# Rotation tables of a state-space scan built once for all groups, and two projections moved behind the scan

## The chip, the core and the metric

The kernel runs on one core of a Trainium2 chip. Its engines have queues of their own, each run in order: TensorE (PE; matmuls), VectorE (DVE; element-wise work and the scan), ScalarE (ACT; copies, casts and functions from tables), GpSimd (POOL; a second element-wise engine) and SyncE (SP; it issues the DMA transfers). Engines wait for each other by semaphores. The metric is device time in microseconds (us) for one execution; lower is better.

## The reference

A hybrid layer is followed by a second block (feed-forward layers, a convolution with an RWKV scan, latent attention), all in fp32 on 512 positions of width 1024. Only the hybrid layer is touched:

```python
proj = jnp.einsum("bld,de->ble", rms_norm(x, pre_g), w_in)
conv_in, z_c, u_s, z_s, g_c, g_s = jnp.split(proj, IN_OFFSETS, axis=-1)
ca, cb = jnp.split(conv_in, 2, axis=-1)
cu = causal_depthwise_conv(ca * jax.nn.sigmoid(cb), conv_w, conv_b)      # 31 taps
cu = jax.nn.silu(layer_norm(cu, conv_ln_g, conv_ln_b))
conv_out = (cu * jax.nn.silu(z_c)) @ w_conv_out
y = jax.nn.gelu(s5_mimo(u_s, ...))       # per group g: s_t = Abar s_(t-1) + Bbar u_t, y = Re(C s) + D u
y = y * jax.nn.sigmoid(y @ w_glu + b_glu)
ssm_out = (y * jax.nn.silu(z_s)) @ w_ssm_out
merged = jax.nn.sigmoid(g_c) * conv_out + jax.nn.sigmoid(g_s) * ssm_out
out = x + rms_norm(merged @ w_out, post_g)
```

The state-space scan (S5) has 32 groups of 16 channels with 64 complex states. Abar is mag * exp(i * angle), with an angle per state and group.

## The kernel before

Activations lie with channels on the 128 partitions and the 512 positions along the free axis. Every weight matrix comes as fp32 and is split into a high and a low part, so that a product is three matmuls. `wload` does this by 1024 columns: SP fetches `raw`, ACT casts it to `wh` (L235), DVE subtracts to get `wl` (L236); there are two buffers of each. `mm3` (L247 to L249) runs xh*wh, xl*wh and xh*wl. One projection, `proj`, is 2048 columns, two halves of 24 matmuls of 512 columns each. The bank of a half is free for the next use when its result has been read.

The hybrid layer is `block1`. Its input projections are named by step in two strings, ORDER_A and ORDER_B, and the steps are issued in that order; a scheduler then places instructions on the engines by priority, in which a step's class (`B1_CLASS`, `B1_PRIO`) can lower it: only the convolutions on ACT and POOL (class C) are lower.

```python
ORDER_A = "p0 P1 T z0 c0 u0 u1 s0 p3 t1 Q0 Q1 q0 c3 P2 t2 s1 Q2 q1 p5 z1 c5 P4 t4 Q3 q2 P6 t6 q3 P7 t7"
ORDER_B = "z2 z3 y0 g0 g1 g2 y1 y2 y3 g3 G L g4 g5 g6 S0 g7 S1 C0 C1 C2 C3 C4 C5 C6 C7"
```

- p and P: a projection of 128 gated convolution channels. After p the convolution runs as c on ACT (a product with each tap, L758) and POOL (its addition, L759). After P the gated result `cp` (DVE, L718) is split into `cph` (ACT, L724) and `cpl` (DVE, L725), and t runs the convolution on PE as a Toeplitz product of 4 weight chunks, 24 matmuls of 256 columns each (L741 to L743).
- u: the scan's input, stored to DRAM by SP and read back as `us` in the layout of the scan. s and z: the gates z_s and z_c, a projection with Silu (z at L792). Both kinds of gate and the squares of x at the start take buffers of a pool `b1z`.
- T (`s5_tables`): quantities of all 32 groups, 32 elements per partition each, among them the powers of Abar and, for the rotation, cosine and sine of the angle times 2^i, by doubling eight times with ten instructions each (L462 to L475; `s5x` and `s5t` are its tiles).
- Q (`s5_pre`), for a quarter q of 8 groups: outer products on POOL (`t`, `w`, L503 and L506), the rotation tables `rc` and `rsn` (cosine and sine of k times the angle for k below 64: six doublings of six DVE instructions, L521 to L526, with 8 to 256 elements), transposes (PE, L531), the kernel of the first 8 steps (PE, L540, then `kt`), the diagonal D added to `kt` group by group (DVE, L545), and 16 transfers that place `kt` in `tz`.
- q (`s5_main`): `us` from DRAM, product with `m` (PE, L571), rotation by the tables (DVE, L577 to L579), the scan (L581), rotation back (L583 on PE, L587 to L589 on DVE), product with `tz` and `w` (PE, L593 and L594).
- Behind the scan: y (gelu), g (gates), G (the product with w_glu), L (layer norm of the convolution, gate z_c), S and C (output products).

Of the kernel before, what the change touches and what calls it, by code (L numbers as in the profile page):

```python
# [341 lines left out]
def s5_tables(P, mp):  # L342
# [119 lines left out]
    for i in range(8):  # L462
        w, u1, u2 = tmp(), tmp(), tmp()
        c2, s2 = (small(), small()) if i >= 2 else (tmp(), tmp())
# [4 lines left out]
        tt(u1, c2, c2, ALU.mult)  # L469
        tt(u2, s2, s2, ALU.mult)  # L470
        tt(w, u1, u2, ALU.add)
        V.tensor_scalar(out=w, in0=w, scalar1=-0.5, scalar2=1.5, op0=ALU.mult, op1=ALU.add)
# [1523 lines left out]
```

## Time and profile before

| | us |
|---|---|
| median of 3 runs | 2741.04 (2734.41 to 2743.03) |
| profiled execution, its own time | 2744.4 |
| span of its trace | 2742.7 |
| PE busy | 2610.5 (95% of the span) |
| DVE busy | 1447.9 (53%) |
| ACT busy | 950.4 (35%) |
| POOL busy | 511.4 (19%) |

The page cuts the span in 40 slices of 68.6 us and gives each engine's busy share in tenths; a window gives busy us between two times. A row of a timeline has the start, the duration, the engine, line and operation, and in brackets the idle time of the engine before it and what ended that. A group of a line has the count, the busy us, the mean ns, and the idle time before. PEclk and the number behind the engines in a window are the granted TensorE clock, as a share of full. The names and lines are those of the kernel before.

### The profile page before, as it was taken

What the parts mean: (1) busy time and instruction counts of PE and PEld (TensorE: products, weight loads), DVE (VectorE), ACT (ScalarE), POOL (GpSimd) and SP (SyncE); (2) the same over time, 40 slices, a digit from 0 to 9 for tenths busy, and PEclk for the clock granted to TensorE, in tenths of its full rate; (3) what the DMA queues carried; (4) which work ended last, traced back from release to release, by engine and by line L of the source; (5) the groups of instructions that cost most, each with busy time, mean ns of one, the idle gap of its engine ahead of it and who ended that gap; (6) DMA issues with size and microseconds to landing.
All of it is one profiled execution on the core that took longest, in us unless ns stands there. A gap on an engine that the chain in (4) does not pass through costs nothing.

```text
span 2742.7 us, 32329 instructions
## 1 busy us (share of the span) xinstructions
PE 2610.5 (95%) x12836; PEld 2092.4 (76%) x12836; DVE 1447.9 (53%) x2064; ACT 950.4 (35%) x1351; POOL 511.4 (19%) x382
## 2 busy tenths in 40 slices
PE   6688799998999999999999999999999999999999
PEld 4567678886888876787678888888888666788887
DVE  9967643636434448743464344443444755643443
ACT  4354444434222343222242233322233454432231
POOL 5687501014000044332010000100001221100000
PEclk8889799998999999999999999999999889999999
DMA  3222232332233342213222332322324312132323
GB/s 111 74 85 90 74 124 88 108 115 70 95 96 102 96 139 72 64 57 106 67 85 95 98 99 91 102 95 90 107 84 138 112 41 62 50 100 87 106 95 105
DMA packets 116071, 251.87 MB, mean 92 GB/s; under 512 B 44176, under 2 KB 53008, under 8 KB 115920
## 3 DMA queue, kind: packets, MB, share of 16 engines
q1 hardware_dynamic: 115664, 249.00, 28.9%
q8 instruction: 100, 1.64, 0.3%
q0 software_dynamic: 256, 0.81, 0.1%
q14 instruction: 51, 0.42, 0.1%
HBM read 235.21 MB, written 13.37 MB: 91 GB/s over the span
## 4 chain that ended last, share of the span: by engine, by line
PE 82%; DVE 12%; DMA 1%; issue 1%; ACT 1%; POOL 1%; SPq 1%; DVEq 0%; ACTq 0%; POOLq 0%
PE bank L247 23%; PE bank L249 23%; PE bank L248 23%; PE bank L1871 2%; DVE wl L236 2%; DVE s5x L357 1%; POOL acc L264 1%; SPq L548 1%; PE bank L1423 1%; PE bank L1227 0%; DVE ra L525 0%; PE bank L742 0%; PE bank L743 0%; DMA s<-nd 0%; DVE rc L523 0%
## 5 line engine op out<-in xcount | busy, mean ns | idle before, releaser
L235 ACT CAST wh<-raw 128x1024 fp32r<-128x1024 f32 (+1 forms) x452 | 437.2, 969 | 1268.1 <-PE bank L248 948.4
L249 PE MATMUL bank<-xh,wl 128*128 128x512 f32 (+1 forms) x2144 | 843.0, 394 | 30.0 <-DVE wl L236 30.0
L248 PE MATMUL bank<-xl,wh 128*128 128x512 f32 (+1 forms) x2144 | 842.8, 393 | 15.6 <-DVE xl L925 6.9
L247 PE MATMUL bank<-xh,wh 128*128 128x512 f32 (+1 forms) x2144 | 838.2, 392 | 18.5 <-ACT wh L235 7.8
L236 DVE TENSOR_TENSOR wl<-raw,wh 128x1024 fp32r<-128x1024 f32 (+1 forms) x418 | 481.9, 1154 | 484.3 <-ACT wh L235 482.9
L249 PEld LDWEIGHTS bank<-xh,wl 128*128 128x128 f32 x2144 | 408.9, 191 | 125.6 <-DVE wl L236 33.7
L247 PEld LDWEIGHTS bank<-xh,wh 128*128 128x128 f32 x2144 | 408.0, 191 | 109.2 <-ACT wh L235 11.7
L248 PEld LDWEIGHTS bank<-xl,wh 128*128 128x128 f32 x2144 | 408.5, 191 | 106.2 <-DVE xl L925 7.8
L264 POOL TENSOR_TENSOR acc<-acc,sq 128x512 f32<-128x512 f32 x54 | 81.4, 1507 | 1326.9 <-ACT sq L263 1325.8
L249 PE MATMUL bank<-mh,wl 128*128 128x512 f32 x704 | 274.6, 390 | 0.0
L248 PE MATMUL bank<-ml,wh 128*128 128x512 f32 x704 | 274.3, 390 | 0.0
L247 PE MATMUL bank<-mh,wh 128*128 128x512 f32 x704 | 274.1, 389 | 0.0
L323 DVE TENSOR_TENSOR up<-bank,rs 128x512 f32<-128x512 f32 x88 | 60.8, 691 | 266.8 <-PE bank L249 266.8
L249 PEld LDWEIGHTS bank<-mh,wl 128*128 128x128 f32 x704 | 132.1, 188 | 33.2 <-DVE wl L236 1.7
L319 DVE TENSOR_TENSOR gp<-bank,rs 128x512 f32<-128x512 f32 x88 | 60.8, 691 | 179.7 <-PE bank L249 179.7
L248 PEld LDWEIGHTS bank<-ml,wh 128*128 128x128 f32 x704 | 132.1, 188 | 27.9
L247 PEld LDWEIGHTS bank<-mh,wh 128*128 128x128 f32 x704 | 132.2, 188 | 25.6
L759 POOL TENSOR_TENSOR xa<-xa,cw 128x512 f32<-128x512 f32 x90 | 129.1, 1435 | 55.1 <-ACT cw L758 52.5
L236 POOL TENSOR_TENSOR wl<-raw,wh 128x1024 fp32r<-128x1024 f32 x34 | 82.8, 2435 | 145.6 <-ACT wh L235 145.1
L758 ACT ACTIVATE cw<-cu,hcw 128x512 f32<-128x512 f32 x90 | 63.7, 720 | 37.5 <-POOL xa L759 37.3
L253 ACT CAST mh<-m 128x512 fp32r<-128x512 f32 x88 | 54.9, 625 | 61.5 <-DVE m L325 61.5
L1871 PE MATMUL bank<-s,s 128*128 128x256 f32 (+3 forms) x192 | 71.6, 431 | 0.4 <-ACT s L1878 0.4
(651 smaller groups left out, 3032.9 us busy)
## 6 DMA issues: line engine op xcount, KB each, us to landing
raw<-in_ffn_gu_dram SPq DMA_DIRECT2D x176, 512.0 KB, 3.4
raw<-in_ffn_dn_dram SPq DMA_DIRECT2D x64, 512.0 KB, 3.6
raw<-in_w_in_dram SPq DMA_DIRECT2D x46, 512.0 KB, 3.5
raw<-in_even_in_dram SPq DMA_DIRECT2D x26, 512.0 KB, 3.6
raw<-in_ffn_dn_dram SPq DMA_DIRECT2D x64, 192.0 KB, 3.2
raw<-in_conv_dram SPq DMA_DIRECT2D x20, 512.0 KB, 3.8
xa<-in_xT_dram SPq DMA_DIRECT2D x16, 256.0 KB, 4.1
raw<-in_w_co_dram SPq DMA_DIRECT2D x8, 512.0 KB, 3.3
```

Source lines behind the costliest of these rows:

```text
L235: nc.scalar.copy(h[:, :m], raw[:, :m])
L236: self.wlo.tensor_tensor(out=l[:, :m], in0=raw[:, :m], in1=h[:, :m].bitcast(F32), op=ALU.subtract)
L247: self.nc.tensor.matmul(ps, h[i][:, s], xh[k], start=a, stop=False)
L248: self.nc.tensor.matmul(ps, h[i][:, s], xl[k], start=False, stop=False)
L249: last = self.nc.tensor.matmul(ps, l[i][:, s], xh[k], start=False, stop=b)
L253: self.nc.scalar.copy(hi, src)
L264: nc.gpsimd.tensor_tensor(out=acc, in0=acc, in1=sq, op=ALU.add)
L319: nc.vector.tensor_tensor(out=gp, in0=pg, in1=rs, op=ALU.mult)
L323: nc.vector.tensor_tensor(out=up, in0=pu, in1=rs, op=ALU.mult)
L758: A.activation(w, cu[:, j:j + T], AF.Copy, scale=hcw[:, 31 * k + j:31 * k + j + 1])
L759: GP.tensor_tensor(out=y, in0=y, in1=w, op=ALU.add)
L1871: MM(ps[:, 0:N], x, y, start=m == 0, stop=False)
```

## The change

The doubling of the base angles goes. In its place the angle r (with its sign) is multiplied by 8, 16, ... 256 in six small copies on ACT, reduced to one turn in eight DVE instructions on all six at once, and given to Sin twice. The rotation tables of all 32 groups are built by a new step R, `s5_rot`, once, in two tiles of 2048 elements: six doublings, the later ones in parts of 512 elements, 42 DVE instructions where the four quarters had 144. The diagonal is spread once into `idd`, and each half quarter adds it in one instruction (8 instead of 32). In the orders, z0 and z1 leave ORDER_A and stand at the head of ORDER_B; steps in ORDER_A are rearranged around R0. The pool `b1z` has 4 buffers instead of 8 and the pool of the later steps, `b1z2`, 8 instead of 4; `s5x` has 8 instead of 12.

```diff
@@ s5_tables
-    ssn = small()
-    V.tensor_scalar(out=ssn, in0=sn, scalar1=sgn, scalar2=None, op0=ALU.mult)
-    rot = []
-    c, s = cs, ssn
-    for i in range(8):
...
-        tt(u1, c, c, ALU.mult)
-        tt(u2, s, s, ALU.mult)
-        tt(c2, u1, u2, ALU.subtract)
-        V.scalar_tensor_tensor(out=s2, in0=c, scalar=2.0, in1=s, op0=ALU.mult, op1=ALU.mult)
...
-        tt(c2, c2, w, ALU.mult)
-        tt(s2, s2, w, ALU.mult)
...
+    rsg = small()
+    V.tensor_scalar(out=rsg, in0=r, scalar1=sgn, scalar2=None, op0=ALU.mult)
+    ang, nn, aa = (P.t(n)[:, 0:192].rearrange("p (i g) -> p i g", i=6) for n in ("ang", "nn", "aa"))
+    for i in range(6):
+        nc.scalar.activation(ang[:, i], rsg, AF.Copy, scale=2.0 ** (i + 3))
+    V.tensor_scalar(out=nn, in0=ang, scalar1=1.0 / TWO_PI, scalar2=MAGIC, op0=ALU.mult, op1=ALU.add)
+    V.tensor_scalar(out=nn, in0=nn, scalar1=MAGIC, scalar2=None, op0=ALU.subtract)
+    for cst in (PI_C1, PI_C2, PI_C3):
+        V.scalar_tensor_tensor(out=ang, in0=nn, scalar=-cst, in1=ang, op0=ALU.mult, op1=ALU.add)
+    V.tensor_scalar(out=ang, in0=ang, scalar1=PI_CLAMP, scalar2=-PI_CLAMP, op0=ALU.min, op1=ALU.max)
+    V.scalar_tensor_tensor(out=aa, in0=ang, scalar=-1.0, in1=ang, op0=ALU.mult, op1=ALU.max)
+    rs6, rc6 = (sm.tile([128, 6, 32], F32, name=n) for n in ("rs6", "rc6"))
+    nc.scalar.activation(rs6, ang, AF.Sin)
+    nc.scalar.activation(rc6, aa, AF.Sin, scale=-1.0, bias=halfpi)
+    rot = [(rc6[:, i], rs6[:, i]) for i in range(6)]
+    idd = sm.tile([16, 32, 16], F32, name="idd")
...
+def s5_rot(P, tb):
+    V = P.nc.vector
+    c, s = (P.q4.tile([128, 2048], F32, name=n).rearrange("p (g k) -> p g k", g=32) for n in ("rc", "rsn"))
+    V.memset(c[:, :, 0:1], 1.0)
+    V.memset(s[:, :, 0:1], 0.0)
+    ta, tb_ = P.t("ra"), P.t("rb")
+    for i in range(6):
+        m = 1 << i
+        n = min(32, 512 // m)
+        for g0 in range(0, 32, n):
+            g = slice(g0, g0 + n)
+            cq, sq = (a[:, g].unsqueeze(2).to_broadcast([128, n, m]) for a in tb["rot"][i])
+            A, B = (x[:, 0:n * m].rearrange("p (g k) -> p g k", g=n) for x in (ta, tb_))
+            V.tensor_tensor(out=A, in0=c[:, g, 0:m], in1=cq, op=ALU.mult)
+            V.tensor_tensor(out=B, in0=s[:, g, 0:m], in1=sq, op=ALU.mult)
+            V.tensor_tensor(out=c[:, g, m:2 * m], in0=A, in1=B, op=ALU.subtract)
+            V.tensor_tensor(out=A, in0=s[:, g, 0:m], in1=cq, op=ALU.mult)
+            V.tensor_tensor(out=B, in0=c[:, g, 0:m], in1=sq, op=ALU.mult)
+            V.tensor_tensor(out=s[:, g, m:2 * m], in0=A, in1=B, op=ALU.add)
+    tb["cs"] = c, s
@@ s5_pre
-    for i in range(6):
-        m = 1 << i
...
-        RE.tensor_tensor(out=A, in0=c[:, :, 0:m], in1=cq, op=ALU.mult)
...
-            V.scalar_tensor_tensor(out=kt[:, i, 0:16], in0=P.ident[0:16, 0:16], scalar=tb["dd"][:, g:g + 1],
-                                   in1=kt[:, i, 0:16], op0=ALU.mult, op1=ALU.add)
+        g4 = slice(8 * q + 4 * hf, 8 * q + 4 * hf + 4)
+        V.tensor_tensor(out=kt[:, :, 0:16], in0=kt[:, :, 0:16], in1=tb["idd"][:, g4], op=ALU.add)
@@ block1
-        zp = E(tc.tile_pool(name="b1z", bufs=8))
+        zp = E(tc.tile_pool(name="b1z", bufs=4))
...
-        pools["z"] = E(tc.tile_pool(name="b1z2", bufs=4))
+        pools["z"] = E(tc.tile_pool(name="b1z2", bufs=8))
...
-ORDER_A = "p0 P1 T z0 c0 u0 u1 s0 p3 t1 Q0 Q1 q0 c3 P2 t2 s1 Q2 q1 p5 z1 c5 P4 t4 Q3 q2 P6 t6 q3 P7 t7"
-ORDER_B = "z2 z3 y0 g0 g1 g2 y1 y2 y3 g3 G L g4 g5 g6 S0 g7 S1 C0 C1 C2 C3 C4 C5 C6 C7"
+ORDER_A = "p0 P1 T c0 u0 u1 p3 c3 Q0 t1 s0 R0 P2 Q1 t2 q0 p5 c5 s1 Q2 P4 q1 t4 Q3 P6 q2 t6 P7 q3 t7"
+ORDER_B = "z0 z1 z2 z3 y0 g0 g1 g2 y1 y2 y3 g3 G L g4 g5 g6 S0 g7 S1 C0 C1 C2 C3 C4 C5 C6 C7"
```

What the scheduler makes of it is shown at three places. In these rows a name's number is the tile's, and the lines of the changed kernel are one to three higher (L462 to L471 and L498 to L503 are new code there).

On ACT, where the convolution of the first pair begins (`xa` is its sum, `cw` a tap's product, `ang` the scaled angles); before:

```order
L755 ACTIVATE xa<-cu,vec,hcw 128x512
L758 ACTIVATE cw<-cu,hcw 128x512 x2
L235 CAST wh<-raw 128x1024
L792 ACT_TABLE_LOAD
L792 ACTIVATE zc<-bank_73 128x512
L724 CAST cph<-cp 128x2x256
L758 ACTIVATE cw<-cu,hcw 128x512
L235 CAST wh<-raw 128x1024
L792 ACTIVATE zc<-bank_74 128x512
```

and changed:

```order
L757 ACTIVATE xa<-cu,vec,hcw 128x512
L760 ACTIVATE cw<-cu,hcw 128x512 x2
L462 ACTIVATE ang<-s5t_495 128x32 x6
L760 ACTIVATE cw<-cu,hcw 128x512
L726 CAST cph<-cp 128x2x256
L235 CAST wh<-raw 128x1024 x2
L470 ACT_TABLE_LOAD
L470 ACTIVATE rs_513<-ang 128x192
```

The results of z0 (`zc`) are gone from here, the scaled angles stand ahead of `cph`, and both next halves of weights stand behind it.

On DVE, where the first rotation tables begin; before (`d` is the scan's decay, spread over the steps):

```order
L521 TENSOR_TENSOR ra<-rc,s5t_530 128x8
L522 TENSOR_TENSOR ra<-rsn,s5t_531 128x8
L558 COPY d_1395<-s5t_491 128x512
L523 TENSOR_TENSOR rc<-ra 128x8 x2
L524 TENSOR_TENSOR ra<-rsn,s5t_530 128x8
L236 TENSOR_TENSOR wl<-raw,wh 128x1024
L525 TENSOR_TENSOR ra<-rc,s5t_531 128x8
```

and changed:

```order
L498 TENSOR_TENSOR ra<-rc,rc_514 128x32
L499 TENSOR_TENSOR rb<-rsn,rs_513 128x32
L560 COPY d_1477<-s5t_491 128x512
L500 TENSOR_TENSOR rc<-ra,rb 128x32
L501 TENSOR_TENSOR ra<-rsn,rc_514 128x32
L502 TENSOR_TENSOR rb<-rc,rs_513 128x32
L236 TENSOR_TENSOR wl<-raw,wh 128x1024
```

The tables of quarters 0 and 1 ran here side by side, 8 elements for each of two; now one set for all groups starts, 32 elements at a time.

On DVE again, at quarter 2 of the scan; before, in the middle of its tables:

```order
L526 TENSOR_TENSOR rsn<-ra 128x8x8
L521 TENSOR_TENSOR ra<-rc,s5t_590 128x8x16
L522 TENSOR_TENSOR ra<-rsn,s5t_591 128x8x16
L236 TENSOR_TENSOR wl<-raw,wh 128x1024
L523 TENSOR_TENSOR rc<-ra 128x8x16
L524 TENSOR_TENSOR ra<-rsn,s5t_590 128x8x16
L525 TENSOR_TENSOR ra<-rc,s5t_591 128x8x16
```

and changed, the whole way from the decay of quarter 2 to its scan:

```order
L560 COPY d_2213<-s5t_491 128x512
L236 TENSOR_TENSOR wl<-raw,wh 128x1024 x3
L547 TENSOR_TENSOR kt<-kt,idd 16x4x16
L236 TENSOR_TENSOR wl<-raw,wh 128x1024
L720 SCALAR_TENSOR_TENSOR cp<-vb,bank_73 64x256 x4
L579 TENSOR_TENSOR vr<-bank_78,rsn 128x512
L580 TENSOR_TENSOR vs<-vs,rc 128x512
L727 TENSOR_TENSOR cpl<-cp,cph 128x2x256
```

No table stands between weight splits any more, and `cp` now stands ahead of the scan's rotation.

## Rows read from the trace of the kernel before

**Rows 1.** Page, part 2: busy tenths in 40 equal slices of the span.
```profile
PE   6688799998999999999999999999999999999999
...
DVE  9967643636434448743464344443444755643443
```

**Rows 2.** Windows: stretch, busy time of each engine (instructions), granted clock, DMA.
```profile
0.00:140.00 140.00, 94.02 (x342) 69.11 (x343) 134.34 (x296) 61.84 (x87) 87.92 (x75) 0.84 0.29 95
140.00:330.00 190.00, 153.58 (x839) 129.82 (x837) 131.71 (x169) 95.39 (x138) 145.50 (x116) 0.85 0.30 87
330.00:400.00 70.00, 61.60 (x347) 54.50 (x348) 31.67 (x41) 26.96 (x39) 2.58 (x2) 0.86 0.34 105
400.00:600.00 200.00, 198.52 (x872) 163.03 (x870) 96.22 (x113) 80.22 (x107) 18.32 (x10) 1.00 0.31 106
```

**Rows 3.** PE's timeline: start, duration, operation, idle time before it and its releaser.
```profile
130.42 0.80 PE L249 MATMUL bank<-xh,wl 128*128 128x512 f32 x1 [12.15 <-DVE wl L236]
...
213.28 0.58 PE L743 MATMUL bank<-cph,wl 128*128 128x256 f32 x1 [9.47 <-DVE wl L236]
...
290.57 0.58 PE L741 MATMUL bank<-cph,wh 128*128 128x256 f32 x1 [9.00 <-ACT cph L724]
...
327.40 0.87 PE L571 MATMUL bank<-us,m 128*128 128x64 f32 x3 [4.47 <-DMA us<-u_dram]
...
369.92 0.58 PE L741 MATMUL bank<-cph,wh 128*128 128x256 f32 x1 [5.81 <-ACT cph L724]
```

**Rows 4.** DVE's groups by line and shape, 0 to 420: count, busy us, mean ns.
```profile
L236 DVE TENSOR_TENSOR wl<-raw,wh 128x1024 fp32r<-128x1024 f32 x54 | 76.1, 1409 | 81.0 <-ACT wh L235 81.0
L545 DVE SCALAR_TENSOR_TENSOR kt<-ident,s5d,kt 16x16 f32<-16x16 f32 x32 | 13.2, 465 | 9.6 <-ACT kt L542 9.5
L357 DVE TENSOR_TENSOR s5x<-s5x 128x32 f32<-128x32 f32 x22 | 12.3, 580 | 0.3
...
L525 DVE TENSOR_TENSOR ra<-rc,s5t 128x8 f32<-128x8 f32 x4 | 5.0, 1261 | 0.0
L579 DVE TENSOR_TENSOR vs<-vs,vr 128x512 f32<-128x512 f32 x4 | 5.6, 1410 | 0.1
...
L578 DVE TENSOR_TENSOR vs<-vs,rc 128x512 f32<-128x512 f32 x4 | 4.1, 1016 | 0.0
...
L808 DVE TENSOR_TENSOR p<-p,y 128x512 f32<-128x512 f32 x4 | 2.8, 690 | 0.1
```

**Rows 5.** Timelines of DVE and POOL at the tables of quarters 2 and 3.
```profile
189.38 1.23 DVE L521 TENSOR_TENSOR ra<-rc,s5t 128x8 f32<-128x8 f32 x1
190.53 0.16 DVE L522 TENSOR_TENSOR ra<-rsn,s5t 128x8 f32<-128x8 f32 x1
...
217.83 0.43 DVE L526 TENSOR_TENSOR rsn<-ra 128x256 f32<-128x256 f32 x1
...
219.37 1.64 POOL L759 TENSOR_TENSOR xa<-xa,cw 128x512 f32<-128x512 f32 x1 [7.42 <-ACT cw L758]
```

**Rows 6.** Timelines of ACT and POOL at the squares of x and a table load.
```profile
16.02 0.61 ACT L663 ACTIVATE sq<-xa 128x512 f32<-128x512 f32 x1
...
60.47 1.28 ACT L792 ACT_TABLE_LOAD   x1
...
8.81 11.46 POOL L665 TENSOR_TENSOR sqa<-sqa,sq 128x512 f32<-128x512 f32 x7 [4.20 <-ACT sq L663]
```

**Rows 7.** PE's timeline where t1 begins, around P6, before P7, at the end.
```profile
143.78 0.28 PE L741 MATMUL bank<-cph,wh 128*128 128x256 f32 x1
...
311.56 0.48 PE L247 MATMUL bank<-xh,wh 128*128 128x512 f32 x1
...
322.54 0.39 PE L249 MATMUL bank<-xh,wl 128*128 128x512 f32 x1
...
352.95 0.48 PE L247 MATMUL bank<-xh,wh 128*128 128x512 f32 x1
...
385.00 0.29 PE L743 MATMUL bank<-cph,wl 128*128 128x256 f32 x1
```

More of the change, by code (lines that the diff above doesn't have):

```diff
@@ L353, in tmp @@
     def tmp(m=1):
-        return sm.tile([128, m, 32] if m > 1 else [128, 32], F32, name="s5x", tag=f"s5x{m}", bufs=12 if m == 1 else 4)
+        return sm.tile([128, m, 32] if m > 1 else [128, 32], F32, name="s5x", tag=f"s5x{m}", bufs=8 if m == 1 else 4)
     def tt(out, a, b, op, e=V):
@@ L457, in s5_tables @@
     tt(mg8, mg8, mg8, ALU.mult)
-    ssn = small()
-    V.tensor_scalar(out=ssn, in0=sn, scalar1=sgn, scalar2=None, op0=ALU.mult)
-    rot = []
-    c, s = cs, ssn
-    for i in range(8):
-        w, u1, u2 = tmp(), tmp(), tmp()
-        c2, s2 = (small(), small()) if i >= 2 else (tmp(), tmp())
-        tt(u1, c, c, ALU.mult)
-        tt(u2, s, s, ALU.mult)
-        tt(c2, u1, u2, ALU.subtract)
-        V.scalar_tensor_tensor(out=s2, in0=c, scalar=2.0, in1=s, op0=ALU.mult, op1=ALU.mult)
[L469 to L472, printed above, removed]
-        tt(c2, c2, w, ALU.mult)
-        tt(s2, s2, w, ALU.mult)
-        c, s = c2, s2
-        if i >= 2:
-            rot.append((c, s))
+    rsg = small()
[14 more added lines that the diff above has]
+    idd = sm.tile([16, 32, 16], F32, name="idd")
+    tt(idd, P.ident[0:16, 0:16].unsqueeze(1).to_broadcast([16, 32, 16]), dd.unsqueeze(2).to_broadcast([16, 32, 16]), ALU.mult)
     prr, nspr = small(8), small(8)
@@ L484, in s5_tables @@
     V.tensor_copy(perm[:, 64:128], P.ident[:, 0:64])
-    return dict(bc=bc, bb=bb, bbs=bbs, dd=dd, prr=prr, nspr=nspr, spr=spr, npi=npi, mg8=mg8, rot=rot, perm=perm)
+    return dict(bc=bc, bb=bb, bbs=bbs, idd=idd, prr=prr, nspr=nspr, spr=spr, npi=npi, mg8=mg8, rot=rot, perm=perm)
+def s5_rot(P, tb):
[18 more added lines that the diff above has]
+    tb["cs"] = c, s
 def s5_pre(P, tb, q):
@@ L542, in s5_pre @@
         nc.scalar.copy(kt.rearrange("p g s -> p (g s)"), ps[0:16, :])
-        for i in range(4):
-            g = 8 * q + 4 * hf + i
-            V.scalar_tensor_tensor(out=kt[:, i, 0:16], in0=P.ident[0:16, 0:16], scalar=tb["dd"][:, g:g + 1],
-                                   in1=kt[:, i, 0:16], op0=ALU.mult, op1=ALU.add)
+        g4 = slice(8 * q + 4 * hf, 8 * q + 4 * hf + 4)
+        V.tensor_tensor(out=kt[:, :, 0:16], in0=kt[:, :, 0:16], in1=tb["idd"][:, g4], op=ALU.add)
         for j in range(8):
             nc.sync.dma_start(tz[16 * j:16 * j + 16, 4 * hf:4 * hf + 4, 16 * j:128], kt[:, :, 0:128 - 16 * j])
-    tb[q] = w2, m1, tz, c, s
+    tb[q] = w2, m1, tz
 def s5_main(P, tb, q, u_dram, y_dram):
@@ L555, in s5_main @@
     gs = slice(8 * q, 8 * q + 8)
-    w2, m1, tz, c, s = tb[q]
+    w2, m1, tz = tb[q]
+    c, s = (a[:, gs] for a in tb["cs"])
     d0 = P.t("d0").rearrange("p (g k) -> p g k", g=8)
@@ L790, in zc_ @@
             for a, ps in enumerate(proj(12 + i)):
-                z = (z_ if i < 2 else y_)("zc")
+                z = y_("zc")
                 A.activation(z, ps, AF.Silu)
@@ L849, in ln @@
                 TT(out=yc[k], in0=yc[k], in1=zc[k], op=ALU.mult)
-                f = z_ if k < 4 else y_ if k < 6 else c
+                f = z_ if k < 2 else y_ if k < 6 else c
                 a, b = f(f"cah{k}", R), f(f"cal{k}", R)
@@ L867, in block1 @@
                 "Q": lambda q: s5_pre(P, tb, q), "q": lambda q: s5_main(P, tb, q, u_dram, y_dram),
-                "T": lambda i: tb.update(s5_tables(P, None)), "G": lambda i: glu(), "S": ssm, "L": lambda i: ln(),
+                "T": lambda i: tb.update(s5_tables(P, None)), "R": lambda i: s5_rot(P, tb), "G": lambda i: glu(), "S": ssm, "L": lambda i: ln(),
                 "C": cout}
```

16 lines of the change are left out of this document (1 added, 15 removed).

## Prediction, made before the changed kernel was run

> **What bounds the kernel now.** Read the page's slices first [rows 1]: TensorE (PE) is busy nine tenths or more almost everywhere, and only the first six or so slices of 68.6 us are not; there VectorE (DVE) is at its fullest and the granted clock of PE is below full. The change touches only that stretch. The table of windows prices it [rows 2]. From 0 to 140 us DVE is busy 134.34 of 140 us and PE 94.02; from 140 to 330 PE is busy 153.58 of 190, from 330 to 400 61.60 of 70, and from 400 to 600 198.52 of 200 at clock 1.00. So PE stands still for 46 + 36 + 8 = 90 us before 400, and its mean clock there is about 0.85, so that of 309 busy us some 40 to 46 are time that the lower level (1.2 instead of 2.4 GHz) costs. Behind about 385 us PE is the bound: work put there costs its full length, and work taken from before it helps only if PE's end of the stretch moves.
>
> The waits say who holds PE up [rows 3]. In the first part it is wl on DVE, 12.15 us at 130.42 the longest. Later it is a chain: 9.47 us on wl, 9.00 and 5.81 on cph, 4.47 on the transfer us. The 9.47 at 213.28 is not a slow wl: that instruction stands in DVE's queue between the rotation tables of quarter 2, from 189.38 to 218.26 [rows 5]. The cph of 290.57 likewise waits for cp, which DVE runs behind the tables of quarter 3.
>
> **What goes.** DVE groups of 0 to 420 us [rows 4]: the base angles' doubling is 80 small instructions, s5x<-s5x 12.3 us for 22, and the other 58, on the same line or near it and of the same size, at 0.33 on average, another 19: some 31 us. The tables are 4 x 36 = 144 instructions; from 1.26 us (128x8, L525, the dearest) to 0.43 where POOL is silent (128x256 at 217.83 [rows 5]), on a mean of 0.58, 84 us. The diagonal is 32 instructions, 13.2 us. Together about 129 us, of which nearly all lies where DVE or a chain through DVE ends last.
>
> **What comes.** s5_rot is 42 instructions on DVE: six each of 32, 64, 128 and 256 elements, and 18 of 512. A small one takes 0.16 us alone and about 1.2 when it meets a POOL instruction (190.53 against 189.38 [rows 5]; the mean of L525 at 128x8 is 1.26 [rows 4]); one of 256 takes 0.43 alone and one of 512 0.69 (L808), 1.02 and 1.41 beside POOL (L578, L579) [rows 4]. All alone: 24 x 0.25 + 18 x 0.69 = 18 us. Half of the small ones blocked, in turn like those two, and large ones at the mean of L578 and L579: 24 x 0.7 + 18 x 1.2 = 38 us. I take 28. Angle reduction: eight DVE instructions of 192 elements, by the neighbours 0.3 to 1.3 us each, say 6. idd and eight kt additions of 64 elements: 9 x 0.35 = 3. So 129 - 28 - 6 - 3 leaves DVE some 90 us lighter. ScalarE (ACT) gets six copies of 32, about 0.2 us each, and two Sin, and the tables it must hold change twice more, 2 x 1.283 us [rows 6]. These 5 us lie ahead of wh, so they are in the estimate below and not free.
>
> Two neighbours of one size that take 1.23 and 0.16 us [rows 5] look like waiting for the end of a POOL instruction, which lasts 1.64 by the seven additions of rows 6. The Trainium skill, page "SBUF — State Buffer", section "SBUF: two separate sides", says that a DVE instruction with two SBUF inputs and a GpSimd instruction take a shared port pair as an exclusive lock for the whole instruction; the trace agrees (0.16 against 1.23 us). By that rule alone every one of the 42 could wait for a whole POOL instruction, and the sum would be that of rival (1) instead of the one below; it speaks against gathering the tables where POOL is busy.
>
> **First stretch.** z0 was filler: its 48 matmuls of 512 at P6's length, 311.56 to 322.93 = 11.4 us [rows 7], stood on PE between P1 and u0. Now u0 follows, and for u1's first half wh stands behind cph, which waits for cp on DVE: PE waits there some 10 us, to about 73.8 (before, PE had z0 to do and the table of rows 6 was z0's). From there DVE counts: 6 for angles, 9 wl of 1.41 [rows 4] = 12.7, 28 of tables, 2.5 of others, 49 in sum; with 3 us of waits for wh, the weight split for s0 starts at about 126. By then p0, P1, u0, u1, p3 and t1 are through, t1 for about the time of one projection. Before, the trace has p0, P1, z0, u0, u1, s0, p3 done when t1 starts at 143.78 [rows 7]. Leaving z0 aside, the same PE work is done 18 us sooner.
>
> **Second stretch.** What is left: seven projections, s0 P2 p5 s1 P4 P6 P7, x 11.4 = 80 us; four blocks of a scan quarter with a toeplitz, which took 311.56 - 290.57 = 21.0 and 352.95 - 327.40 = 25.6 [rows 3, 7] where the tables were done. With the next quarter's transposes and kernel products I take 26, just above both: 104. PE then waits for cph four times; 5.81 at 369.92 has no tables ahead of it, so such waits stay, and with cp now ahead of the scan's operations I take 3.5 each, 14 us. 126 + 80 + 104 + 14 = 324, instead of 385.1 where the stretch ends [rows 7]. The scan's own chain (L577 to L589 on DVE) is not shortened; toeplitz chunks lie between its steps as they already did in quarters 2 and 3.
>
> **What is paid back.** z0 and z1 go to the front of the next part, where PE is full at clock 1.00 [rows 2]: 2 x 11.4 = 22.8 us, in full. They cannot be hidden there. The queues that the two steps are moved past lose their four weight transfers and their splits from the crowded stretch and gain them where DVE is busy 96 of 200 us and ACT 80 [rows 2], so there they cost nothing beyond PE. Halving the pool of z buffers makes the four last squares of x wait for additions on POOL: the seven additions run back to back from 8.81 to 20.27 us, 1.64 each, so the one that the last square needs is through at 15.4, and that square ran at 16.02 [rows 6]: nothing, covered by 0.6 us, and up to 1.6 if the cover is gone. POOL keeps the same convolutions, 90 additions, and its end is needed only by the norm behind 460 us. Sum: 385.1 - 324 - 22.8 = 38 us. The profiled execution took 2744.4 us (span 2742.7), so 2706; the median is 3.4 lower, so **2703**.
>
> **Rivals.** (1) *The tables are blocked throughout*: 24 x 1.0 + 18 x 1.64 (a whole addition of POOL [rows 6]) = 54 us instead of 28, s0 26 us later, the end at 350: gain 12, 2729. For it: quarter 2's 36 instructions, with few others among them, took 28.9 us beside POOL [rows 5]. Against it: POOL itself pauses whenever ACT's products are late (7.42 us idle before 219.37 [rows 5]), and the tables run in the gaps. (2) *The chain, not DVE's load, sets the pace; slower.* Place: the waits for cph and us in the second stretch. cp, cph and cpl are a chain DVE-ACT-DVE in queues that hold convolution products and weight splits; the scan waits for u and its strips by DMA. If only the two waits behind tables go, 9.47 and 9.00 less the 5.81 that remain without tables, the gain is 12.7 us; the z projections that filled waiting PE time leave holes and cost 22.8 at the back: 10 us slower, 2751. It decides from an end of the stretch later than 385.1 - 22.8 = 362.3. Against it: before 140 DVE has no idle time to speak of, which is load and no chain. (3) *More comes free*: tables at 18 us, cph never late, PE at the upper clock in the blocks (21.0 and 3 for transposes each): 116 + 80 + 4 x 24 + 6 = 298, gain 64, 2677. For it: the clock is 0.85 only because PE stands still so often. (4) *In balance*: the tables cost about what (1) says and cph waits stay at 6 us: the end at 357 to 366, within 8 us of before.
>
> **How the numbers follow.** The forecast, an end between 308 and 342 (gain 20 to 54), 0.56; (1) 0.12; (3) 0.15; (4) 0.08; (2) 0.09. A measurement here tells some 0.3%, 8 us, from no change. Faster by more: 0.56 + 0.15 + 0.12, less a little for the edge of (1) = 0.82; within: 0.09; slower: 0.09. The range takes in (1) and the inner part of (3): 2674 to 2738; it leaves out (2), half of (4) and the far end of (3), together under 0.2.
>
> **What would show it.** Right: DVE under 90% busy between 75 and 140; 42 table instructions with a sum of 20 to 40 us; no wait of PE over 7 us for wl behind 75; one new wait of about 10 us for wl or wh near 64 to 74; a stretch that ends near 324, then two projections with Silu and no gap. Wrong: a table sum over 50 us beside full POOL (1); waits for cph of 6 us and more at each quarter with DVE idle (2); s0 after 145, or an end after 362. If the end is right and the total is not, something behind it (norm, gates) moved, which I hold for unlikely, as the order there is the same.

## The result, and the profile after

The changed kernel takes 2702.63 us (median of 4 runs, 2700.72 to 2707.25); the kernel before took 2737.72 in the runs beside it (4 runs, 2733.59 to 2743.03). The ratio is 0.9873, 95% interval 0.9849 to 0.9898: 35 us faster. The prediction was 2703, and its size of the gain 38.

The two slices that answer [rows 1], page part 2 of the changed kernel (busy tenths in 40 slices, now of 67.5 us):

```profile
PE   6798999989999999999999999999999999999999
...
DVE  9955636545434468643654344443444755643442
```

PE's second, third and fifth slices are fuller (7, 9 and 9 instead of 6, 8 and 7). DVE's third, fourth and sixth are lighter (5, 5 and 3 instead of 6, 7 and 4); its seventh is heavier (6 instead of 3). The windows that answer [rows 2] (stretch, busy us of PE, weight loads, DVE, ACT and POOL with instructions, granted clock, DMA):

```profile
0.00:140.00 140.00, 98.25 (x400) 74.41 (x401) 125.30 (x193) 66.92 (x101) 89.24 (x76) 0.87 0.32 104
140.00:330.00 190.00, 167.28 (x966) 143.30 (x965) 106.94 (x87) 102.68 (x145) 157.89 (x116) 0.92 0.32 93
330.00:400.00 70.00, 70.00 (x311) 57.95 (x310) 25.83 (x29) 28.09 (x41) 1.29 (x1) 1.00 0.37 119
400.00:600.00 200.00, 190.88 (x882) 158.67 (x881) 108.51 (x134) 86.16 (x122) 31.68 (x23) 0.97 0.31 101
```

DVE is down from 134.3 to 125.3 us in the first window and from 131.7 to 106.9 in the second. PE does 966 matmuls instead of 839 in the second; its idle time before 400 is 42 + 23 + 0 = 65 us instead of 90, and the granted clock is 0.87, 0.92 and 1.00 where it was 0.84, 0.85 and 0.86. In the last window PE shows 191 us instead of 199; that is the next stage, which begins earlier.

PE's longer waits, which answer [rows 3] and [rows 7] (start, duration, operation, idle time before it and releaser):

```profile
68.82 0.80 PE L247 MATMUL bank<-xh,wh 128*128 128x512 f32 x1 [4.52 <-ACT wh L235]
...
107.70 0.58 PE L745 MATMUL bank<-cph,wl 128*128 128x256 f32 x1 [8.73 <-DVE wl L236]
...
124.70 0.39 PE L745 MATMUL bank<-cph,wl 128*128 128x256 f32 x1 [4.12 <-DVE wl L236]
...
132.12 0.79 PE L249 MATMUL bank<-xh,wl 128*128 128x512 f32 x1 [2.12 <-DVE wl L236]
...
230.89 1.22 PE L577 MATMUL bank<-vs,perm 128*128 128x512 f32 x1 [6.69 <-ACT vs L575]
...
277.81 0.58 PE L744 MATMUL bank<-cpl,wh 128*128 128x256 f32 x1 [1.73 <-DVE cpl L727]
...
329.63 0.40 PE L247 MATMUL bank<-xh,wh 128*128 128x512 f32 x1
```

Two waits for wl of 12.15 and 9.47 us and two for cph of 9.00 and 5.81 have become two for wl of 8.73 and 4.12 and shorter ones; of the scan's only one is long, 6.69 for vs. The last row is the first matmul of z0 behind the last toeplitz. In the kernel before, the first matmul behind the last toeplitz (there it is z2's) is

```profile
385.12 0.40 PE L247 MATMUL bank<-xh,wh 128*128 128x512 f32 x1
```

So the stretch ends at 329.63 instead of 385.12, 55.5 us sooner. Counted from the end of the program, the 9800th matmul, which lies behind z0 and z1 in both, stands at 711.2 us instead of 744.8: 33.6 us sooner. So z0 and z1 took back 55.5 - 33.6 = 21.9.

The two traces' spans differ by 42.4 us, not 33.6. The other 8.8 come later, in stages that have the same instructions in the same order, in steps of 1 to 5 us where the lower clock lasted longer in the one execution or the other (the granted clock from there to the end is 0.98 before and 0.99 in the changed kernel); the profiled execution of before (2744.4) lies 6.7 us above its median of 2737.72, that of the changed kernel (2702.08) at its own. Experiments are therefore read both by the medians and by the end of the stretch. The kernel before was run again beside each group of experiments, and its medians lie between 2733.57 and 2737.72; so a difference of two medians from different groups is good to about 4 us.

### The profile page after: what moved, and what is told of

It is laid out like the page before. It is cut to its first block, busy times and chain, and to the rows that moved or that the text cites. A ratio compares the mean times of both kernels' runs of the same rounds, so it can differ in the third digit from the quotient of the medians.

```text
span 2700.3 us, 32142 instructions
## 1 busy us (share of the span) xinstructions
PE 2595.2 (96%) x12836; PEld 2080.7 (77%) x12836; DVE 1399.5 (52%) x1860; ACT 954.6 (35%) x1361; POOL 523.8 (19%) x382
## 3 DMA queue, kind: packets, MB, share of 16 engines
q8 instruction: 100, 1.64, 0.3%
HBM read 235.21 MB, written 13.37 MB: 92 GB/s over the span
## 4 chain that ended last, share of the span: by engine, by line
PE 83%; DVE 9%; POOL 2%; issue 2%; ACT 2%; DMA 1%; SPq 0%; DVEq 0%; ACTq 0%; POOLq 0%
PE bank L247 24%; PE bank L249 24%; PE bank L248 23%; PE bank L1872 2%; DVE wl L236 2%; POOL xa L761 1%; PE bank L744 1%; ACT wh L235 1%; PE bank L1228 1%; PE bank L745 1%; POOL acc L264 1%; PE bank L743 1%; PE bank L1424 1%; DMA raw<-in_ffn_dn_dram 0%; DVE xl L270 0%
## 5 line engine op out<-in xcount | busy, mean ns | idle before, releaser
L236 DVE TENSOR_TENSOR wl<-raw,wh 128x1024 fp32r<-128x1024 f32 (+1 forms) x418 | 497.1, 1190 | 518.1 <-ACT wh L235 509.3
L249 PEld LDWEIGHTS bank<-mh,wl 128*128 128x128 f32 x704 | 132.1, 188 | 33.6 <-DVE wl L236 2.0
L761 POOL TENSOR_TENSOR xa<-xa,cw 128x512 f32<-128x512 f32 x90 | 137.2, 1525 | 26.7 <-ACT cw L760 23.8
```

Source lines behind the costliest of these rows:

```text
L236: self.wlo.tensor_tensor(out=l[:, :m], in0=raw[:, :m], in1=h[:, :m].bitcast(F32), op=ALU.subtract)
L249: last = self.nc.tensor.matmul(ps, l[i][:, s], xh[k], start=False, stop=b)
L761: GP.tensor_tensor(out=y, in0=y, in1=w, op=ALU.add)
```

## The experiments

All stand against the changed kernel (2702.63; end of the stretch 329.63; sum of the table instructions 39.2 us) but the first, which stands against the kernel before (2734.97 in the runs beside it; 385.12; 85.0). The sum of the table instructions adds up their durations one by one.

| | median, us | end of stretch | tables, us (instructions) |
|---|---|---|---|
| z alone moved, from before | 2737.31 | 359.31 | 77.3 (144) |
| tables per quarter | 2712.31 | 340.61 | 81.1 (144) |
| tables twice over | 2725.11 | 352.30 | 75.7 (84) |
| first convolution cut | 2689.43 | 312.80 | 29.7 (42) |
| old angles | 2713.10 | 340.90 | 38.1 (42) |
| old diagonal | 2705.96 | 334.35 | 43.4 (42) |
| old order | 2714.67 | 339.22 | 43.6 (42) |
| eight columns by Sin | 2702.58 | 323.67 | 33.1 (24) |
| base angles in PSUM | 2696.28 | 319.58 | 27.4 (42) |
| both of these | 2688.48 | 313.21 | 20.3 (24) |
| z0 in its old place | 2711.29 | 348.19, with z0 in it | 41.4 (42) |
| six t buffers | 2701.55 | 329.58 | 41.6 (42) |

### z0 and z1 alone

```diff
-ORDER_A = "p0 P1 T z0 c0 u0 u1 s0 ... p5 z1 c5 ..."
-ORDER_B = "z2 z3 ..."
+ORDER_A = "p0 P1 T c0 u0 u1 s0 ... p5 c5 ..."
+ORDER_B = "z0 z1 z2 z3 ..."
```

> The kernel before with one part of the change alone: z0 and z1 stand behind the scan (with the pools that this needs), the tables stay as they were. My theory: the stretch up to the last toeplitz is held up by DVE and by chains through it, and z0 and z1 filled some of PE's waiting, so the stretch gets shorter by less than their 22.5 us, some 10 to 18 (end at 367 to 375 instead of 385), and the whole 5 to 13 us slower than before, 2743 to 2751. Rival, that the move itself brings the gain by taking four weight splits out of the crowded stretch: end below 362, whole faster than before by up to 20 us.

Measured: ratio to before 1.0001 (0.9987 to 1.0015), no change, where I had expected 5 to 13 us slower. The stretch ends 25.8 us sooner and z0 and z1 take back 21.5 behind it; the two traces are 4.3 us apart at the 9800th matmul. So neither theory held: the move costs what it brings. PE's timeline of this run, its longest wait of the first part and z0's first matmul:

```profile
117.71 0.79 PE L249 MATMUL bank<-xh,wl 128*128 128x512 f32 x1 [13.37 <-DVE wl L236]
...
359.31 0.40 PE L247 MATMUL bank<-xh,wh 128*128 128x512 f32 x1
```

The wait for wl that stood at 130.42 with 12.15 us [rows 3] stands at 117.71 with 13.37: 12.7 us sooner and no shorter. z0 had stood ahead of that wait and did not fill it: PE had been idle 46.0 us up to the wait's end before and 44.1 now. Up to it DVE had worked 124.95 us before and 112.58 now. Two weight splits less are 3.4 us of that; the table instructions are another 6.3, of which 42 instead of 48 had run by then, at 0.43 us each instead of 0.51.

### z0 back in its old place, and its control

```diff
-ORDER_A = "p0 P1 T c0 u0 u1 ..."
-ORDER_B = "z0 z1 z2 z3 ..."
+ORDER_A = "p0 P1 T z0 c0 u0 u1 ..."
+ORDER_B = "z1 z2 z3 ..."
...
-                tc.tile_pool(name="b1t", bufs=8) as tp,
+                tc.tile_pool(name="b1t", bufs=6) as tp,
```

> The changed kernel with z0 in its old place behind the tables' step (six buffers of the t pool instead of eight, to make room). My prediction took z0 for filler there, work that PE did while it waited: then it is nearly free there, and the whole is 6 to 11 us faster than the changed kernel, 2692 to 2697. Against that, the kernel before with z0 and z1 moved had a stretch shorter by 25.6 us for 22.5 paid behind it: by that, z0 costs in its old place what it costs behind the scan, whole 2699 to 2708.

> The changed kernel with six instead of eight buffers of the t pool and nothing else, the control for z0 in its old place. If the two buffers are not missed, the whole is 2699 to 2706 and the end of the stretch within 3 us of 329.6, and what z0 in its old place cost (7 to 9 us) is z0's own. Rival, that the missing buffers cost it: 2707 to 2714, and then z0's place is neutral or better.

Measured: 2711.29, 8.7 us above the changed kernel (four runs, 2703.12 to 2716.77), and 6.4 us later at the 9800th matmul; the median lies above what either theory gave. The buffers alone make 2701.55 and an end at 329.58, nothing. With lighter DVE, z0 in its old place costs more than behind the scan, not less: it is no filler.

### The tables per quarter again

```diff
-def s5_rot(P, tb):
...
+    for i in range(6):
+        m = 1 << i
+        cq, sq = (a[:, gs].unsqueeze(2).to_broadcast([128, 8, m]) for a in tb["rot"][i])
+        V.tensor_tensor(out=A, in0=c[:, :, 0:m], in1=cq, op=ALU.mult)
...
```

> The changed kernel with the rotation tables built per quarter again (144 instructions inside the four quarters), all else as changed (angles by scaling, diagonal in one step, z behind). My theory: 40 to 45 us more of DVE, half of it ahead of the first quarter, half ahead of the cp and weight splits of quarters 2 and 3; end of the stretch at 345 to 355 instead of 329.6, whole 15 to 25 us above the changed kernel, 2718 to 2728. Rival, that the tables were hidden and the angles, diagonal and order brought the gain: at most 6 us above, 2702 to 2709.

Measured: 2712.31, 9.7 us above the changed kernel (at the 9800th matmul 9.0), between the two. PE's two long waits in this run:

```profile
203.81 0.79 PE L249 MATMUL bank<-xh,wl 128*128 128x512 f32 x1 [13.25 <-DVE wl L236]
...
271.28 0.79 PE L249 MATMUL bank<-xh,wl 128*128 128x512 f32 x1 [11.46 <-DVE wl L236]
```

They are the waits for wl behind the tables of quarters 2 and 3, like that of 213.28 in [rows 3], so the place is right. The size was off. The tables' sum is 42 us more, but all of DVE's instructions together sum to only 28.9 us more (busy, with overlaps counted once, 1423.5 instead of 1399.5, page part 1). The same 350 weight splits take 10.8 us less: of the 43 up to the end of the stretch 17 take over 1.5 us, where the changed kernel has 30 that do, beside POOL. The end of the stretch is 11.0 us later.

### All table work twice

```diff
-    for i in range(6):
+    for i in [k for k in range(6) for _ in range(2)]:
```

> The changed kernel with each of the six doublings of the tables done twice over (84 instructions instead of 42, same values). My theory: DVE's load sets the first stretch, so the tables' sum goes from 39 to some 75 us, the first weight split behind them from 130 to about 160, and the whole to 2725 to 2738. Rival, that the chain of cph and us sets the pace and DVE has slack there: first split shifts, but the end of the stretch by under 10 us, whole 2703 to 2712.

Measured: 2725.11, 22.5 above the changed kernel; the sum 75.7, the end 22.7 later. DVE's load does set the first stretch: 36.5 us more of table instructions cost 22.7, six tenths.

### The old angles, the old diagonal, the old order

```diff
# old angles: in s5_tables
-    nc.scalar.activation(rs6, ang, AF.Sin)
...
+    for i in range(8):
+        tt(u1, c, c, ALU.mult)
...
# old diagonal: in s5_pre
-        V.tensor_tensor(out=kt[:, :, 0:16], in0=kt[:, :, 0:16], in1=tb["idd"][:, g4], op=ALU.add)
+        for i in range(4):
+            V.scalar_tensor_tensor(out=kt[:, i, 0:16], in0=P.ident[0:16, 0:16], scalar=tb["dd"][:, g:g + 1],
...
# old order
-ORDER_A = "p0 P1 T c0 u0 u1 p3 c3 Q0 t1 s0 R0 P2 Q1 t2 q0 p5 c5 s1 Q2 P4 q1 t4 Q3 P6 q2 t6 P7 q3 t7"
+ORDER_A = "p0 P1 T c0 u0 u1 s0 p3 t1 Q0 R0 Q1 q0 c3 P2 t2 s1 Q2 q1 p5 c5 P4 t4 Q3 q2 P6 t6 q3 P7 t7"
```

> The changed kernel with the base angles doubled eight times on DVE as before (80 small instructions; tables at once, diagonal, z and order as changed). It gives DVE back some 31 us less the 5 to 8 us that scaling and reduction take. Doubling all table work gave 36 us of DVE and cost 21 to 23 us, 0.6 per us; by that theory this costs 12 to 18 us, whole 2714 to 2721. Rival, that these instructions lie where DVE or PE waits anyway: at most 5 us, 2702 to 2708.

> The changed kernel with the diagonal added group by group as before (32 instructions instead of 8 and the spread). DVE theory at 0.6 us per us: 13.2 us against 7.4 + 0.7, so 0 to 4 us, whole 2702 to 2707. Rival, that the diagonal holds the chain of the placing transfers and so the scan: 8 us and more, 2710 and above.

> The changed kernel with the steps of the first string in the order of before (z0 and z1 taken out, the table step behind Q0). Moving z alone gave nothing and tables per quarter cost 9 to 10 us of the 35; if angles and diagonal bring 12 to 20, 5 to 12 are left for the new order of s0, p3, c3 and the P steps: whole 2707 to 2715. Rival, that the order is neutral: 2700 to 2705.

Measured: 2713.10, 2705.96 and 2714.67. The angles cost 10.5 us when put back (11.3 by the end of the stretch), a little under the range and well over the rival. The diagonal cannot be told from nothing: 3.3 by the median, 4.7 at the end of the stretch, 2.2 at the 9800th matmul and 0.2 at the end of the trace. The old order costs 12 us by the median, 9.6 at the end of the stretch and 8.7 at the 9800th matmul. Where, PE's timeline of that run shows:

```profile
107.39 0.80 PE L249 MATMUL bank<-xh,wl 128*128 128x512 f32 x1 [10.75 <-DVE wl L236]
...
243.60 0.58 PE L743 MATMUL bank<-cph,wh 128*128 128x256 f32 x1 [7.06 <-ACT cph L726]
...
286.57 0.66 PE L596 MATMUL bank<-sh,w 128*128 128x64 f32 x2 [7.08 <-DVE sh L591]
```

The wait for cph is back (7.06 us): in the old order t4 follows P4 directly, and PE has only transposes to do until cph is there, while in the new one the quarter q1 stands between (P4 q1 t4). The scan's `sh` holds PE for 7.08 us: its last addition stands in DVE's queue behind a weight split and cp (281.13 to 285.05 us), and no toeplitz matmuls lie between the steps of that quarter, as they do in the changed kernel. The wait for wl in the first part is 10.75 instead of 8.73.

### POOL's part in the price of a table instruction

```diff
# first convolution cut
-                for j in range(1, 31):
+                for j in range(1, 31 if k else 2):
```

> The changed kernel without taps 2 to 30 of the first convolution on ACT and POOL (29 products on ACT and 29 additions on POOL are left out), so that POOL has mostly the outer products beside the tables. If the tables' small instructions cost 1.2 us because each waits for a POOL instruction, more of them take 0.2 to 0.4 now and the 42 sum to 22 to 32 us instead of 39, the additions of 512 to 0.69 each once POOL is silent; whole 5 to 20 us faster, 2683 to 2698. Rival, that 1.2 us is the instruction's own cost at this place (waits on the weight halves, its own pipeline): the sum stays at 37 to 41.

Measured: 2689.43 (four runs, 2683.06 to 2705.27), and the sum 29.7 us. DVE's timeline in this run:

```profile
81.86 0.20 DVE L498 TENSOR_TENSOR ra<-rc,rc 128x32 f32<-128x32 f32 x1
81.98 0.19 DVE L499 TENSOR_TENSOR rb<-rsn,rs 128x32 f32<-128x32 f32 x1
...
103.25 1.65 DVE L500 TENSOR_TENSOR rc<-ra,rb 128x512 f32<-128x512 f32 x1
```

With POOL silent the instructions of 32, 64 and 128 elements cost 0.2 to 0.3 us, 4.3 us for 18 where the changed kernel has 19.2; those of 512, which now meet the next quarter's outer products on POOL, cost up to 1.9 as ever. The gain of 13 us does not come from the tables alone, since ACT loses 29 products, too.

```diff
# eight columns by Sin: in s5_tables
-    for i in range(6):
-        nc.scalar.activation(ang[:, i], rsg, AF.Copy, scale=2.0 ** (i + 3))
+    for i, f in enumerate((8, 16, 24, 32, 40, 48, 56, 64, 128, 256)):
+        nc.scalar.activation(ang[:, i], rsg, AF.Copy, scale=float(f))
...
+    nc.scalar.activation(s[:, :, 1:8], ang[:, 0:7].rearrange("p k g -> p g k"), AF.Sin)
+    nc.scalar.activation(c[:, :, 1:8], aa[:, 0:7].rearrange("p k g -> p g k"), AF.Sin, scale=-1.0, bias=halfpi)
# in s5_rot
-    for i in range(6):
-        m = 1 << i
+    for i in range(3):
+        m = 8 << i
```

> The changed kernel with the first eight columns of the tables taken from Sin (angles times 8, 16, ... 56 scaled and reduced along with 64, 128 and 256), so that the first three doublings, 18 small instructions that took 19 us between them because POOL blocks them, fall away; ACT gets four more scaled copies and Sin of some 250 elements more. DVE theory at 0.6 us per us: the tables' sum falls from 39 to 19 to 24 us, the first split behind them from 130 to about 117, whole 8 to 14 us faster than the changed kernel, 2689 to 2695. Rival, that cp, cph and wh set the first stretch anyway: within 4 us of the changed kernel.

Measured: 2702.58, nothing by the median, 6.0 us by the end of the stretch. Eighteen instructions that had taken 19.2 us are gone, and the sum falls by 6.1 only. DVE's timeline says why:

```profile
79.18 1.52 DVE L501 TENSOR_TENSOR ra<-rc,rc 128x256 f32<-128x256 f32 x1
80.62 1.52 DVE L502 TENSOR_TENSOR rb<-rsn,rs 128x256 f32<-128x256 f32 x1
...
93.16 1.90 DVE L502 TENSOR_TENSOR rb<-rsn,rs 128x512 f32<-128x512 f32 x1
...
112.06 0.68 DVE L501 TENSOR_TENSOR ra<-rc,rc 128x512 f32<-128x512 f32 x1
```

The instructions of 256 elements, 0.42 each in the changed kernel, now stand where POOL is busy and take 1.5; the first of 512 take 1.5 to 1.9. The blocked time (the time in which an instruction of DVE waits for one of POOL) went over to the next in the queue. So most of the cost is not the instruction's; it is POOL's, paid by the table instruction that happens to run beside it. The rival's number came out by the median, but the run does not test its reason, since the tables hardly got cheaper.

```diff
# base angles in PSUM: in s5_tables, s5_rot and block1
-    rs6, rc6 = (sm.tile([128, 6, 32], F32, name=n) for n in ("rs6", "rc6"))
+    rs6, rc6 = (P.banks[6][:, a:a + 192].rearrange("p (i g) -> p i g", i=6) for a in (0, 192))
...
+    P.rot["sd"] = (P.banks[4:7], [0])
...
+        P.rot["sd"] = (P.banks[4:6], [0])
```

> The changed kernel with the twelve base cosines and sines written by Sin into a PSUM bank instead of SBUF (the side banks are two instead of three until the tables are done), so that four of the six instructions of each doubling have one operand in PSUM, as L579 has (0.68 us each, whatever POOL does), and two still have both in SBUF. If what DVE waits for is a POOL instruction whenever both inputs lie in SBUF: lines of the four kinds take 0.2 to 0.45 us for up to 256 elements and 0.69 for 512, the other two lines keep 1.2 and 1.3 to 1.7; sum 25 to 31 us instead of 39, whole 2 to 8 us faster than the changed kernel, 2695 to 2701. Rival, that any DVE instruction is slow beside POOL: all six lines as before, sum 37 to 44.

> Both together: the first eight columns from Sin and the three base angles left in PSUM. 24 instructions, 16 of them with an operand in PSUM (4 of 0.42 and 12 of 0.69, 10 us) and 8 that can be blocked (up to 1.6, 13 us): sum 18 to 23 us instead of 33 without PSUM and 39 in the changed kernel; end of the stretch 8 to 14 us earlier than in the changed kernel (329.6), whole 2689 to 2697. Rival, that POOL's pauses give back what the blocking takes (POOL waits for ACT, ACT for PE, PE for DVE): the end at 321 to 326, whole 2697 to 2703.

Measured: 2696.28 with the base angles in PSUM, the sum 27.4, both in the expected range; both together 2688.48, the sum 20.3, the end at 313.21, 16.4 us sooner, which is more than expected. DVE's groups by line with the angles in PSUM:

```profile
L503 DVE TENSOR_TENSOR rsn<-ra,rb 128x512 f32<-128x512 f32 x3 | 4.4, 1457 | 0.0
...
L500 DVE TENSOR_TENSOR rc<-ra,rb 128x512 f32<-128x512 f32 x3 | 2.6, 861 | 0.0
...
L502 DVE TENSOR_TENSOR rb<-rc,bank 128x512 f32<-128x512 f32 x3 | 2.0, 680 | 0.0
...
L503 DVE TENSOR_TENSOR rsn<-ra,rb 128x32 f32<-128x32 f32 x1 | 1.3, 1302 | 0.0
...
L502 DVE TENSOR_TENSOR rb<-rc,bank 128x32 f32<-128x32 f32 x1 | 0.2, 209 | 0.0
```

The lines with an operand in `bank` take 0.2 us at 32 elements and 0.68 at 512, while those with both inputs in SBUF beside them take 1.3 at 32, and 0.86 and 1.46 on the mean at 512. The timelines of DVE and POOL show it within one POOL instruction:

```profile
89.63 0.22 DVE L498 TENSOR_TENSOR ra<-rc,bank 128x64 f32<-128x64 f32 x1
...
90.01 0.97 DVE L500 TENSOR_TENSOR rc<-ra,rb 128x64 f32<-128x64 f32 x1
...
89.48 1.42 POOL L525 TENSOR_TENSOR w<-w,tmp 128x576 f32<-128x576 f32 x1
```

While POOL runs from 89.48 to 90.90, the instruction with an operand in PSUM is through in 0.22 us; the one with both inputs in SBUF ends at 90.98, just behind POOL. The Trainium skill, page "SBUF — State Buffer", section "Who interferes with whom", says that a DVE instruction with at most one SBUF input, outside its two-port modes, does not contend with GpSimd; the rows agree (0.209 against 1.302 us at 32 elements). One input in SBUF is not enough by itself, though: the copy of the scan's decay has no more, and waits in the changed kernel (1.73 us on the mean against 0.41 before, rows below). Whether that copy runs in such a mode no run here shows.

The last one is the best version: ratio to before 0.9846 (0.9822 to 0.9871), 45 us, against 0.9873 (0.9849 to 0.9898) of the changed kernel. Against the changed kernel it is 10 us better by the two gains, 45 and 35 us (14 by the medians as they stand), by the traces 16.4 at the end of the stretch and 17.7 at the 9800th matmul; the two intervals overlap a little, since each has its own runs of before. That it is better is clear from the traces; how much of it reaches the end, 10 to 18 us, is not. Its windows:

```profile
0.00:140.00 140.00, 108.28 (x467) 82.65 (x468) 112.20 (x178) 76.83 (x117) 106.92 (x84) 0.91 0.34 112
140.00:330.00 190.00, 170.33 (x971) 145.50 (x970) 112.38 (x101) 105.54 (x153) 148.54 (x109) 0.90 0.35 101
```

DVE is down to 112 us in the first window and PE up to 108.

## Why the prediction was right, step by step

- *The bound, and that only the stretch before 385 us is touched*: right. The table twice over costs 22.7 us there, and the end of the stretch carries the gain. Of the signs for it, DVE is busy 54.4 of 65 us between 75 and 140 (84%, under the 90 asked for), but the sign "no wait of PE over 7 us for wl behind 75" failed: one of 8.73 stands at 107.70.
- *The tables' price, 28 us from 18 to 38*: it was 39.2, above the upper end. Even the upper end had let only half of the 24 small ones wait for POOL; of the 18 with 32 to 128 elements 15 did, and the 24 took 21.8 us instead of 16.8. The 18 of 512 took 17.4 instead of 21.6, since only five of them were blocked. That the upper end is so close is two errors that cancel. The changed kernel's DVE and POOL timelines:

```profile
83.09 1.27 DVE L498 TENSOR_TENSOR ra<-rc,rc 128x32 f32<-128x32 f32 x1
84.28 0.20 DVE L499 TENSOR_TENSOR rb<-rsn,rs 128x32 f32<-128x32 f32 x1
...
87.11 1.23 DVE L501 TENSOR_TENSOR ra<-rsn,rc 128x32 f32<-128x32 f32 x1
...
105.11 0.28 DVE L502 TENSOR_TENSOR rb<-rc,rs 128x128 f32<-128x128 f32 x1
...
114.27 0.68 DVE L503 TENSOR_TENSOR rsn<-ra,rb 128x512 f32<-128x512 f32 x1
...
129.64 2.43 DVE L236 TENSOR_TENSOR wl<-raw,wh 128x1024 fp32r<-128x1024 f32 x1
...
116.91 1.66 POOL L761 TENSOR_TENSOR xa<-xa,cw 128x512 f32<-128x512 f32 x1 [11.87 <-ACT cw L760]
```

From 78 to 105 POOL works without a break and DVE's small instructions take 1.0 to 1.5 us, once 0.2; from there to 116.91 POOL waits for ACT 11.87 us and they run at their own length, 0.28 and 0.68. Rival (1) had the mechanism, but its 54 us, every instruction blocked, was further off than my 28.
- *Angles 6, diagonal and its spread 3*: the angles' instructions of 192 elements, of which there are seven and not eight, took 5.1 us. The diagonal was mis-sized: six of the eight kt additions are blocked, too (two take 0.20 us), 0.92 us on the mean and 7.4 in all, and the spread took 0.7. Groups of DVE, 0 to 420 us, the last from the kernel before:

```profile
L547 DVE TENSOR_TENSOR kt<-kt,idd 16x64 f32<-16x64 f32 x8 | 7.4, 924 | 0.2 <-ACT kt L545 0.2
...
L503 DVE TENSOR_TENSOR rsn<-ra,rb 128x512 f32<-128x512 f32 x3 | 4.0, 1347 | 0.0
...
L236 DVE TENSOR_TENSOR wl<-raw,wh 128x1024 fp32r<-128x1024 f32 x60 | 98.3, 1640 | 141.3 <-ACT wh L235 133.8 <-DMA y_dram<-yq 7.5
...
L560 DVE COPY d<-s5t 128x512 f32<-128x512 f32 x4 | 6.9, 1727 | 0.0
...
L558 DVE COPY d<-s5t 128x512 f32<-128x512 f32 x4 | 1.6, 412 | 0.0
```

So the instructions that were changed take 129 - 39 - 5 - 8 = 77 us less instead of 90. DVE as a whole did not get that much: all its instructions sum to 60 us less, and by the two pages it is busy 48.4 us less (1399.5 instead of 1447.9, overlaps counted once). Here, too, blocked time went over to instructions that nobody had changed. A weight split takes 1.64 us on the mean instead of 1.41 [rows 4], 15.2 us in sum over the same 350 of them, and a copy of the decay 1.73 instead of 0.41, 5.3 us for the four. The prediction priced every instruction that goes and comes and took the rest of DVE's queue as it was; that term is missing from it.
- *A new wait near 64 to 74, because wh stands behind cph*: right in place and cause; PE's waits there were 4.52 us for wh at 68.82 and 1.73 for wl at 72.72, not some 10. ACT's timeline: it waits 10.53 us for cp, then casts cph and the two halves of weights.

```profile
67.20 0.62 ACT L726 CAST cph<-cp 128x512 fp32r<-128x512 f32 x1 [10.53 <-DVE cp L720]
67.72 1.99 ACT L235 CAST wh<-raw 128x1024 fp32r<-128x1024 f32 x2
```

- *s0's weight split at 126*: it starts at 129.64, 3.6 us late, takes 2.43 us beside POOL, and PE has it at 132.12. From 73.84 on the table instructions ahead of it took 37.6 us instead of 28, and DVE waited 5.76 us for wh instead of 3. Against that, all but 0.34 us of the angles' work was done by then, where 6 had been counted, and seven weight splits stood ahead instead of nine.
- *The second stretch, 324 - 126 = 198 us*: 329.63 - 129.64 = 200.0. Its parts came out otherwise, so that the sum fits is in part luck: cph and cpl hold PE hardly at all (1 to 2 us each time, where 14 us had been counted for the four), the scan's `vs` holds it for 6.69 and some 1 us, and the granted clock is 0.92, not full. What each of these cost was not taken apart.
- *z0 and z1 paid back, 22.8*: 21.9 in the trace. But the reason given, that z0 was filler in its old place, is wrong: moving z0 and z1 alone brings 25.8 and takes 21.5 back, and z0 put back costs 6 to 9. Rival (2) rested on the same picture and falls with it: PE's idle time ahead of the long wait did not grow when z0 had gone (46.0 and 44.1 us).
- *The order*: it was in the sum only as 14 us of waits for cph instead of the longer ones. It is a part of its own, 9 to 12 us.
- *The sum*: 38 forecast, 33.6 at the 9800th matmul and 35.1 by the medians. Part by part from the experiments, the medians give 10 for the tables at once, 10 for the angles, 12 for the order, 0 to 3 for the diagonal and 0 for z, 32 to 35 in sum; such parts need not add up, and each is good to about 4 us. That the median came out within 0.4 us is luck: the gain was 3 us too large, and the kernel before was 3 us slower in the three runs shown than in all four. The gain itself is right within its range, with a table price and a DVE load that were both too favourable and an order that was worth more than it had been given.
- *Before the stretch*: the halved z pool did not hold up the squares of x: the last ran at 15.74, and the addition it waits for was through at about 8.46 + 4 x 1.64 = 15.0.

What stays open: a microsecond of DVE work in this stretch does not cost one fixed price. By page part 1 DVE is busy 31.6 us more with the tables twice over, 24.0 with the tables per quarter and 21.2 with the old angles, and the stretch ends 22.7, 11.0 and 11.3 us later: five to seven tenths. Where the rest is taken up was not shown. The trace has one place where the engines hold each other up, POOL's 11.87 us for ACT above, at the end of which ACT had itself waited 12.74 us, until 114.39, for `cu` from DVE; no run took that apart. Why the diagonal's 5 us at the end of the stretch are not there at the end of the program was not tried either, nor why the 6 us of the eight columns by Sin do not show in the median.

## What to carry to other kernels

Before pricing a VectorE instruction, look at what GpSimd does beside it: the same instruction took 0.2 or 1.3 us, and removing some of them handed most of the waiting to the next, here also to instructions of other steps. With one of its two inputs in PSUM an instruction of the tables no longer waited; here that and fewer instructions were worth another 10 to 18 us. Work that stands ahead of a long wait is not filler for it; move it alone before you count on it either way.

## What the runs showed of the hardware that I had not expected

A blocked VectorE instruction ends just behind the GpSimd instruction that ran when it started, and its own size adds little. In the changed kernel each of the 15 blocked ones of 32 to 128 elements ends 0.05 to 0.15 us behind the end of such a GpSimd instruction, and each of the five of 512 elements 0.55 us behind it. So a blocked one took 1.27 us at 32 elements, and with eight columns by Sin 1.52 at 256 and 1.9 at 512 at the worst, against 0.20, 0.42 and 0.69 alone. That the time is so nearly a matter of the other engine's, and goes over to the next instruction when one is taken away (18 instructions less, 19.2 us before, 6.1 us saved), I had not expected; nor that one operand in PSUM takes a line of the same table out of it altogether (0.209 us beside 1.302).
